# The first stage of a hybrid encoder layer in one written order, with 512 columns in a matmul of the dilated values

## The chip, the core and the metric

The kernel runs on one core of one Trainium2 chip. The metric is the device time of the program in microseconds; where several runs are compared, their median counts. Times inside the program come from one profiled execution.

## The reference

One layer of an encoder, for 1024 tokens of 1024 channels, all in float32. What matters here is that every branch starts from one normed input and one projection of it:

```python
h = rmsnorm(x, attn_norm_g)
proj = h @ w_in
(c_q, c_kv, k_rope, z_mla, q_dil, k_dil, v_dil, z_dil, g_mla, g_dil) = jnp.split(proj, split_points, axis=-1)
a_out = mla_attention(c_q, c_kv, k_rope, positions, ...)   # norms c_q and c_kv, then @ w_uq, @ w_ukv, rope, attention of 8 heads
d_out = dilated_mixture(q_dil, k_dil, v_dil, positions)    # 24 heads of 64 columns, three groups of 8
merged = sigmoid(g_mla + b) * ((a_out * silu(z_mla)) @ w_o_mla) + sigmoid(g_dil + b) * ((d_out * silu(z_dil)) @ w_o_dil)
out = rmsnorm(x + merged @ w_out, final_norm_g)
```

`c_q` has 256 columns, `c_kv` 128, `k_rope` 32, and `v_dil` 1536, which are three groups of 512.

## The kernel before, in words

**Precision.** Every float32 product is three matmuls (`mm3`, L144 to L146): high part by high part, high by low, low by high. An operand is cut in two by `split`: ScalarE (ACT in the profile) writes the rounded high part (L150), and VectorE (DVE) or GpSimd (POOL) subtracts it from the operand, which leaves the low part (L151). All DMAs leave through one queue, SyncE's (SP, L140), in program order.

**Stages.** The program has a first stage, then the block products (`blocks`, whose order is written out by hand: 16 items, each with 7 products of 12 matmuls by a Strassen-like scheme on halves of the tokens and of the contraction), then attention, gates and output. Only the first stage and the head of the block products are touched by the change.

**The first stage** consists of these pieces:

- `latent_proj`: `x` transposed comes in 16 loads, is scaled by the norm's gain and cut into high and low parts (`hTh`, `hTl`, which stay for the whole stage); 192 matmuls of 416 columns give `c_q`, `c_kv` and `k_rope` of 8 tiles of 128 tokens (`lat`). ACT sums the squares of the latent columns (L261, L262).
- `tables` computes sine and cosine tables and stores them to DRAM (`s_cs`); `table` loads them again, once for the latent heads (`cs_m`) and once for the dilated ones (`cs_d`).
- `token_factors`: ACT squares `x` in rows (L275), DVE works out the norm's factor of each token (`rcol`, L277), TensorE transposes it for a copy along the free axis (`R`).
- `up_weights` loads `w_uq` in two pieces and `w_ukv` in one through a staging tile `u_raw` that has one buffer, and splits each; the low parts (`uq_l`, `ukv_l`) are subtracted on POOL.
- `latents`, for each half of the tokens: DVE scales the `lat` tiles by the latent norm (L357), TensorE transposes them (L364), ACT and DVE write `lat_h` and `lat_l`, and 60 matmuls of 512 columns give the queries, keys and values of the latent heads. These leave by way of `mla_st` to DRAM.
- `dil_v`, six times (three groups, two quads of heads): one quad has 256 columns, so a token tile takes 8 steps of the contraction by 3 matmuls of 256 columns. The result is scaled by `rcol` on ACT (L445, L456) and DVE (L446) and stored.
- `block_sums`: sums and differences of the parts of `x` for the block products: 16 tiles `y` are loaded again, scaled by ACT (L473), combined on POOL (L475 to L478), and cut by ACT and DVE into `s_h` and `s_l`.

**What sets the order.** Inside the first stage a scheduler orders the instructions of each engine by their dependences and by the sequence in which the pieces are called. The pools have 6 PSUM buffers for `latent_proj` and `dil_v` (`NB_A`) and 2 for `latents`, so that matmuls of `dil_v` stand between those of `latents` on TensorE. At the end of the stage POOL combines the `y` tiles and splits the first operands (`w_l`) of the block products, again in an order that the scheduler chose. From `blocks` on, the order is the one in which the calls are written (`manual_schedule`): the operand of product j is split `LEAD` = 5 products ahead.

## Time and profile before

| | |
|---|---|
| median of three runs | 1254.29 us (1252.39 to 4276.14) |
| the profiled execution, its own time | 1254.46 us |
| its span in the trace | 1252.5 us, so about 2 us lie around it |
| PE busy in the span | 1212.4 us (97%) |
| first stage, until the first block product | 226.88 us |
| PE busy from 45 to 60 us, and from 60 to 80 us | 13.11 of 15 us, 12.50 of 20 us |
| PE busy from 80 to 220 us | all of 140 us |

A row of the timeline has the start and the duration of an instruction in us, its engine, its line in the kernel, the operation, the tiles it writes and reads, and in brackets how long its engine stood idle before it and what ended that. Matmuls overlap one another, so what one costs in a stream is the distance of the starts, not the duration in its row. A row of the groups has the count, the busy time, the mean of one in ns, and the idle time ahead. A row of the windows has, for each stretch, the time, then for each engine the busy time and the count, then TensorE's granted clock and the DMA share.

### The profile page before, as it was taken

To read this page: it belongs to the slowest core of one execution; us is meant where nothing else is said; L and a number is where in the kernel's file an instruction comes from. 1 tells how busy PE (TensorE), PEld (TensorE's weight loads), DVE (VectorE), ACT (ScalarE), POOL (GpSimd) and SP (SyncE) were. 2 spreads that over 40 slices of the span, in tenths; PEclk is the share of its full clock that TensorE was granted. 3 is DMA by queue.
4 is the path that set the end of the run, shared out by engine and by line. 5 is a ranking of instruction groups with operands and counts; after the bars stand their busy time and mean duration, and the time that the engine had idled before them with its cause. 6 is when DMAs were issued, how large, how long until landed. Compare 5 with 4: busy or idle time off the path is not lost.

```text
span 1252.5 us, 19486 instructions
## 1 busy us (share of the span) xinstructions
PE 1212.4 (97%) x6909; PEld 1064.5 (85%) x6909; DVE 730.8 (58%) x1304; ACT 622.0 (50%) x1300; POOL 570.2 (46%) x482
## 2 busy tenths in 40 slices
PE   8979999999999999999999999999999999999998
PEld 8979999888888888888888889878878888888886
DVE  7473534467657653345555575647766767759542
ACT  6534345444343344455554666545655656654232
POOL 2352218877777777543464442415521201168322
PEclk9989999999999999999999999899999999999999
DMA  9847589365445642496887898964634445225241
GB/s 333 225 157 283 196 302 317 103 180 156 135 132 165 174 127 100 122 268 197 233 257 200 207 294 212 266 175 116 178 128 119 110 118 135 85 96 182 84 151 51
DMA packets 126416, 221.37 MB, mean 177 GB/s; under 512 B 28072, under 2 KB 60400, under 8 KB 121392
## 3 DMA queue, kind: packets, MB, share of 16 engines
q1 hardware_dynamic: 126320, 220.14, 59.5%
q8 instruction: 54, 0.88, 0.3%
q14 instruction: 42, 0.34, 0.1%
HBM read 149.24 MB, written 70.85 MB: 176 GB/s over the span
## 4 chain that ended last, share of the span: by engine, by line
PE 75%; DMA 11%; DVE 4%; ACT 4%; issue 3%; POOL 1%; SPq 1%; ACTq 0%; POOLq 0%; DVEq 0%
PE bank L145 5%; PE bank L144 5%; PE bank L146 5%; PE pj L145 4%; PE bank L871 4%; PE pj L144 4%; PE pj L146 4%; DMA at_r<-s_dk 3%; PE st_a L144 2%; PE st_a L145 2%; PE st_d L145 2%; PE st_c L145 2%; PE st_d L146 2%; PE st_a L146 2%; PE st_c L146 2%
## 5 line engine op out<-in xcount | busy, mean ns | idle before, releaser
L151 POOL TENSOR_TENSOR w_l<-w_raw,w_h 128x512 fp32r<-128x512 f32 x188 | 247.5, 1330 | 276.7 <-ACT w_h L150 218.1
L150 ACT CAST w_h<-w_raw 128x512 fp32r<-128x512 f32 x188 | 112.6, 621 | 110.1 <-POOL w_raw L495 92.7
L144 PE MATMUL bank<-at_r,w_h 128*128 128x512 f32 x344 | 142.8, 415 | 0.0
L879 DVE TENSOR_TENSOR at_r<-bank,at_r 128x512 fp32r<-128x512 f32 x128 | 88.0, 688 | 84.5 <-ACT at_r L873 84.2
L145 PE MATMUL bank<-at_r,w_h 128*128 128x512 f32 x344 | 136.6, 397 | 0.6 <-POOL at_r L151 0.6
L146 PE MATMUL bank<-at_r,w_l 128*128 128x512 f32 x344 | 136.7, 397 | 0.0
L873 ACT CAST at_r<-bank 128x512 fp32r<-128x512 f32 x128 | 74.9, 586 | 72.5 <-PE bank L871 71.9
L145 PE MATMUL pj<-w_l,at_r 128*128 128x256 f32 x384 | 109.7, 286 | 0.0
L146 PE MATMUL pj<-w_h,at_r 128*128 128x256 f32 x384 | 109.6, 285 | 0.0
L144 PE MATMUL pj<-w_h,at_r 128*128 128x256 f32 x384 | 109.5, 285 | 0.0
L1137 ACT ACTIVATE at_f<-at_f,at_f 128x256 f32<-128x256 f32 x128 | 64.1, 502 | 52.1 <-DVE at_f L1130 51.8
L1156 DVE TENSOR_TENSOR at_r<-bank,at_r 128x512 fp32r<-128x512 f32 x64 | 43.9, 686 | 70.4 <-ACT at_r L1152 70.3
L495 POOL TENSOR_TENSOR w_raw<-w_raw 128x512 f32<-128x512 f32 x64 | 82.8, 1294 | 0.1
L871 PE MATMUL bank<-consts,at_f 128*128 128x128 f32 x512 | 77.2, 273 | 1.7 <-ACT at_f L863 1.1
L146 PEld LDWEIGHTS bank<-at_r,w_l 128*128 128x128 f32 x344 | 65.7, 191 | 14.9
L146 PEld LDWEIGHTS pj<-w_h,at_r 128*128 128x128 f32 x384 | 74.2, 193 | 1.0
L145 PEld LDWEIGHTS pj<-w_l,at_r 128*128 128x128 f32 x384 | 74.3, 193 | 0.7
L144 PEld LDWEIGHTS pj<-w_h,at_r 128*128 128x128 f32 x384 | 74.2, 193 | 0.7
L145 PEld LDWEIGHTS bank<-at_r,w_h 128*128 128x128 f32 x344 | 65.9, 192 | 9.9 <-POOL at_r L151 1.0
L144 PEld LDWEIGHTS bank<-at_r,w_h 128*128 128x128 f32 x344 | 65.8, 191 | 9.2
L895 PE MATMUL bank<-at_r,at_r 128*128 128x256 f32 x256 | 67.7, 285 | 1.3 <-ACT at_r L873 1.3
L896 PE MATMUL bank<-at_r,at_r 128*128 128x256 f32 x256 | 67.5, 285 | 0.9 <-DVE at_r L879 0.9
(321 smaller groups left out, 3325.3 us busy)
## 6 DMA issues: line engine op xcount, KB each, us to landing
w_raw<-wt SPq DMA_DIRECT2D x48, 512.0 KB, 3.7
at_r<-s_dq SPq DMA_DIRECT2D x32, 512.0 KB, 7.3
s_dk<-dq_st SPq DMA_DIRECT2D x80, 128.0 KB, 2.4
s_dv<-dv_st SPq DMA_DIRECT2D x32, 256.0 KB, 3.0
s_dq<-dq_st SPq DMA_DIRECT2D x64, 128.0 KB, 2.4
zt<-s_gt SPq DMA_DIRECT2D x32, 256.0 KB, 4.5
w_raw<-wv SPq DMA_DIRECT2D x12, 512.0 KB, 5.8
at_r<-s_dk SPq DMA_DIRECT2D x8, 576.0 KB, 11.3
```

Of the source, the lines that this page charges most:

```text
L144: mm(out, lh, rh, start=start, stop=False, skip_group_check=skip)
L145: mm(out, lh, rl, start=False, stop=False, skip_group_check=skip)
L146: return mm(out, ll, rh, start=False, stop=stop, skip_group_check=skip)
L150: self.nc.scalar.copy(out=h, in_=raw)
L151: sub.tensor_tensor(out=l, in0=raw, in1=h.bitcast(F32), op=ALU.subtract)
L495: self.nc.gpsimd.tensor_tensor(out=b[out], in0=b[x], in1=b[y], op=ALU.subtract)
L871: self.nc.tensor.transpose(pt[:, o:o + 128], self.P[k, b][:, 128 * kc:128 * kc + 128], self.ident)
L873: self.nc.scalar.copy(out=h, in_=pt)
L879: self.nc.vector.tensor_tensor(out=l, in0=pt, in1=h.bitcast(F32), op=ALU.subtract)
L895: mm(out, vv[:, kc], ph[:, x], start=kc == 0, stop=False)
L896: mm(out, vv[:, kc], pl[:, x], start=False, stop=kc == 7)
L1137: nc.scalar.activation(out=p, in_=p, func=AF.Exp, scale=-1.0, bias=nm, accum_out=den)
```

## The change

The whole first stage gets a written order as well (`first_stage`, under the same `manual_schedule` as `blocks`).

- **Dilated values.** A group's 512 columns are done at once. The work is 48 parts c = 0 to 47, 16 to a group; a part is 12 matmuls of 512 columns over half of the contraction for one token tile. Four tiles take their first half, then their second half, then the other four tiles; in group g the half whose operands are there comes first. 576 matmuls of 512 columns take the place of 1152 of 256. Each finished tile is taken by one ACT (L504) and one DVE (L505) instruction of 512 columns, and stored by one DMA.
- **Latent heads.** `latents` becomes a generator. From part 7 on, 1.5 of its 37 steps follow each part, and they are through after part 31. `latent_factors` does the norm's factors of all eight tiles at once, and the scalings of `lat` (`latent_scaled`, L387) stand behind parts 2 to 9. `up_weights` is called ahead of the parts, and its low parts are subtracted on DVE. `u_raw` keeps its one buffer. `mla_st` has 5 buffers in place of 2; PSUM is 4 and 4 buffers.
- **Sums behind.** `block_sums` is a generator that runs behind parts 32 to 42: two rounds of loads, then scaling, combining, and splitting of the round before. The `cs_d` tables are loaded at part 36, the first block weights at part 40, and their operands are split at parts 44 to 47.
- **Moved into the block products.** The four multiplications of `cs_d` by `R` on POOL, the four zero fills of `s_dq`, and the second block load. Operands of the block products change their pool every 4 products, not every one.

How this moves instructions is seen best at three places. The first is ACT just after the latent products, where the casts of the up weights stand. Names: `dv_st` is the staging tile of the dilated values, `lat_h` the transposed latents' high part. Before:

```order
L445 ACTIVATE dv_st<-pj,rcol 128x4x64 x5
L150 CAST uq_h<-u_raw 128x768
L445 ACTIVATE dv_st<-pj,rcol 128x4x64
L367 ACTIVATE lat_h<-pj,consts 128x512 x2
L445 ACTIVATE dv_st<-pj,rcol 128x4x64
L150 CAST w_h<-w_raw 128x512 x3
L150 CAST uq_h<-u_raw 128x768
L367 ACTIVATE lat_h<-pj,consts 128x512
```

And now:

```order
L279 ACTIVATE x_in,x_ss<-x_in 128x1024
L251 ACTIVATE x_junk,lat_ss<-pj 128x256
L251 ACTIVATE x_junk,lat_ss<-pj 128x128
L251 ACTIVATE x_junk,lat_ss<-pj 128x256
L251 ACTIVATE x_junk,lat_ss<-pj 128x128
L150 CAST uq_h<-u_raw 128x768 x2
L150 CAST ukv_h<-u_raw 128x1024
L504 ACTIVATE dv_st<-pj,rcol 128x8x64 x4
L406 ACTIVATE lat_h<-pj,consts 128x512 x3
```

The three casts, which stood apart between values that ACT was taking, now stand together, and the first four values (parts 4 to 7) are behind all three.

The second place is DVE at the same time. Before, the latent scalings follow the norm's factors, and the up weights are not on this engine:

```order
L208 SCALAR_TENSOR_TENSOR rs_u<-rs_u,lat_sc 128x8 x2
L209 SCALAR_TENSOR_TENSOR rs_y<-rs_u,rs_y 128x8 x2
L353 TENSOR_TENSOR rs_y<-rs_y,rcol 128x4 x4
L357 TENSOR_SCALAR lat<-lat,rs_y 128x256
L357 TENSOR_SCALAR lat<-lat,rs_y 128x128
```

Now the three subtractions of the up weights stand between them:

```order
L380 TENSOR_TENSOR rs_y<-rs_y,rcol 128x8 x2
L151 TENSOR_TENSOR uq_l<-u_raw,uq_h 128x768 x2
L151 TENSOR_TENSOR ukv_l<-u_raw,ukv_h 128x1024
L387 TENSOR_SCALAR lat<-lat,rs_y 128x256
L387 TENSOR_SCALAR lat<-lat,rs_y 128x128
L387 TENSOR_SCALAR lat<-lat,rcol 128x64
L387 TENSOR_SCALAR lat<-lat,rs_y 128x256
L387 TENSOR_SCALAR lat<-lat,rs_y 128x128
L387 TENSOR_SCALAR lat<-lat,rcol 128x64
L505 SCALAR_TENSOR_TENSOR dv_st<-pj,rcol,dv_st 128x8x64
```

So every scaling of `lat`, which the transposes on TensorE read, is behind the last of the up weights.

The third place is POOL at the end of the stage. Before, the combining of `y` (L475 to L478) and the splits of the first block operands alternate (L495 is a difference of block weights):

```order
L478 TENSOR_TENSOR y_1558<-y_1558,y_1555 128x512
L151 TENSOR_TENSOR w_l<-w_raw,w_h 128x512 x2
L495 TENSOR_TENSOR w_raw<-w_raw 128x512 x2
L151 TENSOR_TENSOR w_l<-w_raw,w_h 128x512 x2
L495 TENSOR_TENSOR w_raw<-w_raw 128x512
L475 TENSOR_TENSOR y_1588<-y_1585,y_1588 128x512
```

Now all 16 combinations come first. The last of them and what follows:

```order
L538 TENSOR_TENSOR y_1769<-y_1767,y_1769 128x512
L539 TENSOR_TENSOR y_1767<-y_1763,y_1767 128x512
L540 TENSOR_TENSOR y_1763<-y_1769,y_1763 128x512
L541 TENSOR_TENSOR y_1765<-y_1765,y_1763 128x512
L151 TENSOR_TENSOR w_l<-w_raw,w_h 128x512 x2
L648 TENSOR_TENSOR w_raw<-w_raw 128x512
L151 TENSOR_TENSOR w_l<-w_raw,w_h 128x512
L648 TENSOR_TENSOR w_raw<-w_raw 128x512
L151 TENSOR_TENSOR w_l<-w_raw,w_h 128x512
```

The operands of the first block products are therefore behind the last sum, where four of them were ahead of the last two rounds of sums.

The diff, cut to its core (added parts of `block_sums` that only repeat what was there are left out):

```diff
-NB_A = 6
+LATENTS_BEGIN, LATENTS_PACE = 7, 1.5
...
-    def latent_proj(self, lp, wl, xp, pj):
+    def first_products(self, lp, wl, xp, pools):
...
+                product(t, kc)
...
+        tables = self.tables(xp)
+        next(tables)
+        self.v_load(0, 0)
+        for i in range(4):
+            self.v_split(0, i)
+        for t in range(3):
+            squares(t)
+        taken(4)
+        next(tables)
+        self.v_load(0, 1)
+        for t in range(3, 5):
+            squares(t)
+        taken(5)
+        next(tables)
+        for t in range(5, 7):
+            squares(t)
+        for i in range(4):
+            self.v_split(1, i)
+        squares(7)
+        for t in range(6, 8):
+            taken(t)
+        run_all(tables)
...
+        v.tensor_copy(self.rcol, y)
...
+    def token_row(self, tp, pp):
...
-            self.split(raw[:, :n], uh[:, i] if i < 2 else kh, ul[:, i] if i < 2 else kl, nc.gpsimd)
+            self.split(raw[:, :n], uh[:, i] if i < 2 else kh, ul[:, i] if i < 2 else kl, nc.vector)
...
+    def latent_factors(self, tp):
...
+    def latent_scaled(self, t):
+        y, c = self.lat_f, self.lat[:, t]
+        for s, f in ((slice(0, 256), y[:, t:t + 1]), (slice(256, 384), y[:, 8 + t:9 + t]), (slice(384, 448), self.rcol[:, t:t + 1])):
+            self.nc.vector.tensor_scalar(out=c[:, s], in0=c[:, s], scalar1=f, scalar2=None, op0=ALU.mult)
...
-
+                    yield
...
+            yield
...
+            def stage():
+                return tp.tile([128, 2, 512], F32R, name="mla_st", bufs=5)
...
+            o = self.rope(pa, up_q(slice(640, 768)), cos, sin, tp)
+            yield
+                if j > 1:
+                    scaled(o[j - 2], self.qr[j - 2])
+                yield
...
-    def dil_v(self, g, quad, tp, pj):
...
+    def v_load(self, g, s):
+        if g == 3:
+            return
+        raws = self.v_raw[s] = [self.wp.tile([128, 2, 2, 256], F32, name="w_raw") for _ in range(2)]
+        for i in range(2):
+            for quad in range(2):
+                self.dma(raws[i][:, :, quad], self.a["wv"][2 * g + quad, s][:, 2 * i:2 * i + 2])
+    def v_split(self, s, i):
+        wp = (self.wp, self.wpx)[s]
+        h = wp.tile([128, 512], F32R, name="w_h", bufs=4)
+        l = wp.tile([128, 512], F32R, name="w_l", bufs=4)
+        self.split(self.v_raw[s][i // 2][:, i % 2].rearrange("p q c -> p (q c)"), h, l, self.nc.gpsimd)
+        self.v_w[s, i] = h, l
+    def v_part(self, c, pool, tp):
+        g, r = divmod(c, 16)
+        part, t = divmod(r, 4)
+        t += 4 * (part // 2)
+        s = (0, 1, 1, 0)[part] ^ (g & 1)
+        begin = part % 2 == 0
+        if begin:
+            self.v_ps[t] = pool.tile([128, 512], F32, name="pj")
+        ps = self.v_ps[t]
+        sl = slice(128 * t, 128 * t + 128)
+        for i in range(4):
+            kc = 4 * s + i
+            self.mm3(ps, self.hTh[:, kc, sl], self.hTl[:, kc, sl], *self.v_w[s, i], begin and i == 0, not begin and i == 3)
+        if begin:
+            return
+        nc = self.nc
+        pv = ps.rearrange("p (h d) -> p h d", d=64)
+        f = self.rcol[:, t:t + 1]
+        if g < 2:
+            st = tp.tile([128, 8, 2, 64], F32R, name="dv_st")
+            nc.scalar.mul(st[:, :, 0], pv, f)
+            nc.vector.scalar_tensor_tensor(out=st[:, :, 1], in0=pv, scalar=f, in1=st[:, :, 0].bitcast(F32), op0=ALU.mult, op1=ALU.subtract)
+            if g == 0:
+                dst = self.dv[0][128 * t + 64:128 * t + 192]
+                dst = self.dv[1].rearrange("(r m) x -> m r x", r=4)[32 * t:32 * t + 32]
+            self.dma(dst, st.rearrange("p h a d -> p (h a d)"))
+        else:
+            st = tp.tile([128, 8, 64], F32, name="dv_st")
+            nc.scalar.mul(st, pv, f)
+            self.dma(self.dv[2][:, 128 * t:128 * t + 128].rearrange("a t x -> t a x"), st.rearrange("p (a h) d -> p a (h d)", h=2))
...
+        loads(0)
+        loads(1)
+        yield
+        scaled(0)
+        yield
+        for kc in range(4):
+            added(kc)
+            if kc:
+                parts(kc - 1)
+                if kc < 3:
+                    loads(kc + 1)
+            yield
+            if kc < 3:
+                scaled(kc + 1)
+            yield
+        parts(3)
+    def first_stage(self, cp, dpool, sums):
+        tc, nc = self.tc, self.nc
+        self.v_raw, self.v_w, self.v_ps, self.blk, self.opd = {}, {}, {}, {}, {}
+        with ExitStack() as ctx, ExitStack() as left, ExitStack() as inner:
+            pool = lambda stack, name, bufs=1, **k: stack.enter_context(tc.tile_pool(name=name, reuse_waits="tile", bufs=bufs, **k))
+            pl = pool(ctx, "pj_l", 4, space=PSUM)
+            pj = pool(ctx, "pj_a", 4, space=PSUM)
+            vp = pool(ctx, "dvp", 3, side="right")
+            lp = pool(left, "lp")
+            with ExitStack() as stack:
+                wl, xp = pool(stack, "wl"), pool(stack, "xp", 3)
+                self.first_products(lp, wl, xp, (pj, pl))
+            mpool, up, tp = pool(left, "cosm"), pool(left, "up"), pool(left, "lt", 2)
+            self.cos_m, self.sin_m = self.table(mpool, "cs_m", 32)
+            self.latent_factors(tp)
+            weights = self.up_weights(up)
+            latents = self.latents(weights, up, tp, pl)
+            steps, later = 0.0, None
+            for c in range(48):
+                self.v_part(c, pj, vp)
+                g, r = divmod(c, 16)
+                if 2 <= c < 10:
+                    self.latent_scaled(c - 2)
+                if c == 20:
+                    self.token_row(vp, pl)
+                first, second = (0, 1) if g & 1 else (1, 0)
+                if r == 6:
+                    self.v_load(g + 1, first)
+                if r == 14:
+                    self.v_load(g + 1, second)
+                if g < 2 and 12 <= r < 15:
+                    for i in ((0, 1), (2,), (3,))[r - 12]:
+                        self.v_split(first, i)
+                if g and r < 3:
+                    for i in ((0, 1), (2,), (3,))[r]:
+                        self.v_split(1 - (g & 1), i)
+                if c >= LATENTS_BEGIN and latents:
+                    steps += LATENTS_PACE
+                    while steps >= 1 and latents:
+                        steps -= 1
+                        try:
+                            next(latents)
+                        except StopIteration:
+                            latents = None
+                            left.close()
+                            sp = pool(sums, "sums")
+                            z = self.zero = sp.tile([128, 512], F32, name="zero")
+                            nc.gpsimd.memset(z, 0.0)
+                            later = self.block_sums(sp, pool(inner, "bs"))
+                elif later:
+                    next(later, None)
+                if c == 36:
+                    self.cos_d, self.sin_d = self.table(dpool, "cs_d", 0)
+                if c == 40:
+                    self.block_loads(0, self.block_items[0], (self.wp, None))
+                if c >= 44:
+                    for j in ((0, 1), (2,), (3,), (4,))[c - 44]:
+                        self.block_minus(j, self.block_items)
+                        self.block_operand(j, self.block_items)
+            run_all(later)
+            self.block_minus(LEAD, self.block_items)
+            for r in (0, S + 64):
+                for p in range(2):
+                    self.dma(self.dk[0][:, p, :, :, r:r + 64].rearrange("h c x t -> (c x) h t"), z[:64].rearrange("p (h t) -> p h t", t=64))
+                self.dma(self.dv[0][r:r + 64].rearrange("r (a b) -> (r a) b", b=512), z)
...
-            wp = (self.wp, self.wpx)[j % 2]
+            wp = (self.wpx, self.wp)[j // 4 % 2]
...
-        for n in range(2):
-            self.block_loads(n, items[n])
-        for i in range(4):
-            self.dma(self.dq[2][i].rearrange("e c r h (a b) f m -> (e c r) (h a) (b f m)", a=2), self.zero.unsqueeze(1).to_broadcast([128, 4, 512]))
-        for j in range(LEAD):
-            self.block_minus(j, items)
-            self.block_operand(j, items)
-        self.block_minus(LEAD, items)
-        with self.tc.manual_schedule():
...
+        self.block_loads(1, items[1], pools)
+        for x in range(1, places + 14):
...
+            if x in (2, 3, 4, 5):
+                y, c = (self.cos_d, self.sin_d)[x // 2 - 1], slice(512 * (x % 2), 512 * (x % 2) + 512)
+                self.nc.gpsimd.tensor_tensor(out=y[:, c], in0=y[:, c], in1=self.R[:, c], op=ALU.mult)
...
+            if x in (4, 8, 12, 16):
+                i = x // 4 - 1
+                self.dma(self.dq[2][i].rearrange("e c r h (a b) f m -> (e c r) (h a) (b f m)", a=2), self.zero.unsqueeze(1).to_broadcast([128, 4, 512]))
...
+                self.first_stage(cp, dpool, sums)
```

288 lines of the change are left out of this document (114 added, 174 removed).

## The prediction

> **What bounds the kernel now.** The page comes first: TensorE is busy almost throughout, and only the first three slices of 40 (31.3 us each) are below 9 for its own reasons.
>
> ```profile
> PE 1212.4 (97%) x6909; PEld 1064.5 (85%) x6909; DVE 730.8 (58%) x1304; ACT 622.0 (50%) x1300; POOL 570.2 (46%) x482
> PE   8979999999999999999999999999999999999998
> ```
>
> So time is won on TensorE alone: fewer or cheaper matmuls, or less standing idle in the first stage. The windows say where it stands (time, then busy time and count of PE, PEld, DVE, ACT, POOL, granted clock, DMA share, GB/s).
>
> ```profile
> 45.00:60.00 15.00, 13.11 (x111) 12.91 (x110) 7.88 (x45) 4.81 (x15) 1.70 (x2) 1.00 1.01 248
> 60.00:80.00 20.00, 12.50 (x85) 12.00 (x84) 14.56 (x44) 5.18 (x10) 7.57 (x6) 0.74 0.36 119
> 80.00:200.00 120.00, 120.00 (x895) 114.83 (x895) 53.97 (x82) 51.64 (x95) 39.61 (x30) 1.00 0.72 257
> 200.00:220.00 20.00, 20.00 (x170) 20.00 (x168) 7.56 (x7) 10.00 (x19) 16.93 (x13) 1.00 0.88 326
> 220.00:240.00 20.00, 19.04 (x108) 16.58 (x107) 8.03 (x7) 10.85 (x23) 15.95 (x11) 1.00 0.47 155
> ```
>
> Between 80 and 220 us nothing is left to fill. The one large hole is at 60 to 80 us. The timeline of PE names the five stops (the last column says how long PE stood and for what) and gives the starts of matmuls from which I take what one costs.
>
> ```profile
> 5.77 0.71 PE L144 MATMUL pj<-wl_h,at_r 128*128 128x416 f32 x1 [5.77 <-ACT wl_h L150]
> 44.15 0.28 PE L144 MATMUL pj<-w_h,at_r 128*128 128x256 f32 x1
> 53.86 0.27 PE L279 MATMUL pj<-consts,rs_y 128*8 128x128 f32 x1 [1.89 <-DVE rs_y L209]
> 71.38 0.69 PE L364 MATMUL pj<-consts,lat 128*128 128x128 f32 x2 [6.81 <-DVE lat L357]
> 73.39 0.47 PE L364 MATMUL pj<-consts,lat 128*128 128x128 f32 x1 [0.69 <-DVE lat L357]
> 80.31 0.60 PE L364 MATMUL pj<-consts,lat 128*128 128x128 f32 x4
> 80.66 0.36 PE L146 MATMUL pj<-w_h,at_r 128*128 128x256 f32 x1
> 213.76 0.28 PE L146 MATMUL pj<-w_h,at_r 128*128 128x256 f32 x1
> 225.64 0.28 PE L146 MATMUL pj<-w_h,at_r 128*128 128x256 f32 x1
> 226.88 0.50 PE L144 MATMUL st_a<-at_r,w_h 128*128 128x512 f32 x1 [0.96 <-ACT dv_s L456]
> 229.74 0.39 PE L144 MATMUL st_b<-at_r,w_h 128*128 128x512 f32 x1
> 232.46 0.39 PE L144 MATMUL st_c<-s_h,w_h 128*128 128x512 f32 x1
> ```
>
> From 213.76 to 225.64 there are 99 matmuls of 256 columns: 0.120 us each. From 229.74 to 232.46 there are 12 of 512: 0.227 each, 2.72 for the twelve. Four transposes take 0.35.
>
> **The budget of the stage before**, from the first value matmul (44.15) to the first block product (226.88), is 182.7 us: 1152 x 0.120 = 138.2 for the values; 120 x 0.227 = 27.2 for the latent heads; 32 transposes 2.8; stops of 1.89 + 6.81 + 0.69 + 0.96 = 10.4; and 4.1 that remain. Of these some 2.5 are a half clock:
>
> ```profile
> 68.00:71.40 3.40, 0.02 (x1) 0.03 (x1) 3.40 (x5) 0.35 (x1) 3.40 (x4) 0.50 0.00 0
> 74.00:76.00 2.00, 2.00 (x11) 2.00 (x10) 2.00 (x9) 0.39 (x1) 0.00 (x0) 0.50 0.00 0
> 77.40:80.00 2.60, 2.60 (x24) 2.60 (x24) 1.38 (x3) 1.77 (x4) 0.80 (x1) 1.00 0.89 282
> ```
>
> After the long stop the granted clock stays at 0.50 for about 5 us of work. By the Trainium skill (TensorE: Matmul & The Clock Gate, on the clock gate) an idle window of some microseconds halves the clock until the array has been busy about as long; these rows agree, with one stop of 6.81 us. A longer stop costs no second such toll.
>
> **The wider matmuls.** 1152 x 0.120 = 138.2 become 576 x 0.227 = 130.6, which is 7.6 us less, all of it on TensorE. Bounds: nothing, if a 512 costs two 256s, and 576 x (0.240 - 0.227) = 7.6 by these rows. I take the rows: the stationary side is a 128 x 128 tile of `at_r` in the values as in the block products. The Trainium skill (same page, Back-to-back issue gap) gives an isolated warm matmul as columns / 2.4 + 2.5 ns; by that a pair of 256 and one 512 differ by 2.5 ns, an estimate of 1.5 us for the whole edit. The measured 0.120 is well over what the formula has for 256, so I follow the row.
>
> **The latent heads' start.** Here the order bites. The latent products end near 44.2 as before. Parts 0 to 7 run to 44.2 + 8 x 2.72 = 65.9. Behind part 7 come the first transposes, and they read `lat` tiles that DVE scales only after all three subtractions of the up weights. `u_raw` has one buffer, so the loads form a ladder: a load, ACT's cast, DVE's subtraction, and only then the next load. Its rungs by the rows of before:
>
> ```profile
> L140 SPq DMA_DIRECT2D u_raw<-wuq x2: 398/412/426, 62.3 to 77.6; - x2
> L150 ACT CAST uq_h<-u_raw x2: 832/836/839, 67.1 to 81.3; 128x768 fp32r<-128x768 f32 x2
> L150 ACT CAST ukv_h<-u_raw x1: 1052/1052/1052, 89.7 to 89.7; 128x1024 fp32r<-128x1024 f32 x1
> DMA to landing us min/median/max: 4.3/4.6/4.8
> L151 DVE TENSOR_TENSOR wl_l<-wl_raw,wl_h 128x416 fp32r<-128x416 f32 x4 | 2.3, 580 | 0.0
> s_qn<-mla_st SPq DMA_DIRECT2D x8, 512.0 KB, 3.0
> 53.84 0.17 DVE L277 COPY rcol<-rs_y 128x8 f32<-128x8 f32 x1
> 56.73 0.36 DVE L349 SCALAR_TENSOR_TENSOR lat_sc<-lat_ss,rcol 128x4 f32<-128x4 f32 x4
> ```
>
> - A DVE subtraction of 768 columns, from the 416-column row by width: 0.58 x 768 / 416 = 1.07; of 1024: 1.43.
> - The first one. `rcol` was there at 54.0 before. In the new order ACT has all squares, four value casts and the sines of the tables ahead of `taken(7)`, and the cosines' store and four loads of `cs_m` are ahead of `u_raw` on SP: I put `rcol` at 57 and the factors at 60.5 (17 small operations of about 0.2). The first load is there by then, and its subtraction ends at 61.5.
> - Two more rungs. Landing between 3.0 (the 512 KB store) and 4.8 (this load before); with little else on the queue I take 3.9. So 3.9 + 0.84 + 1.07 = 5.8, and 3.9 + 1.05 + 1.43 = 6.4: the last subtraction ends at 73.7 (72 to 75.5).
> - Then four scalings of about 1.0 each (16 long and 8 short ones, whose row follows) and two takings of values of 0.7:
>
> ```profile
> 69.89 6.39 DVE L357 TENSOR_SCALAR lat<-lat,rs_y 128x256 f32<-128x256 f32 x16
> L151 DVE TENSOR_TENSOR mla_st<-pj,mla_st 128x512 fp32r<-128x512 f32 x16 | 11.1, 692 | 23.2 <-ACT mla_st L150 23.2
> ```
>
> The transposes can start at S = 73.7 + 4.0 + 1.4 = 79.1. PE is at 65.9, so it **stands 13.2 us** where before it stood 6.81 + 0.69. It cannot go round this: the values of parts 4 to 7 wait on ACT behind the same three casts, and their PSUM buffers are the ones that part 8 needs.
>
> **The rest of the stage.** From S: 40 parts x 2.72 = 108.8; latents 27.2; transposes 2.8; the 4.1 that remained before, half clock included. S + 142.9 = 222.0. The stop for the tokens' transpose (1.89) is gone, since part 20 is long after `rcol`.
>
> **The tail.** The first sums can be loaded when the latents have left their pool, behind part 31, near 179. The rows of before for this chain:
>
> ```profile
> DMA to landing us min/median/max: 3.5/5.8/8.5
> L473 ACT ACTIVATE y<-y,consts x16: 708/720/725, 186.0 to 221.1; 128x512 f32<-128x512 f32 x16
> L477 POOL TENSOR_TENSOR y<-y,y x4: 1301/1624/1694, 192.2 to 223.2; 128x512 f32<-128x512 f32 x4
> L151 DVE TENSOR_TENSOR s_l<-y,s_h 128x512 fp32r<-128x512 f32 x16 | 20.3, 1298 | 27.7 <-ACT s_h L150 27.3
> 182.17 4.32 SPq L140 DMA_DIRECT2D y<-xt  x8
> 189.44 1.30 POOL L475 TENSOR_TENSOR y<-y,y 128x512 f32<-128x512 f32 x1 [5.19 <-ACT y L473]
> ```
>
> From load to first combination 7.3 us: 187. A round on POOL is four operations of 1.30 to 1.62, 6.0; rounds 0 and 1 end at 193 and 199. Rounds 2 and 3 need buffers that DVE's splits free at 194.5 and 200.5, then 5.8 of landing and 2.9 of scaling: combined by 210 and 217. The first block operand then is split by 218.5 and the second by 220, against a TensorE that arrives at 222. That cover is 3.5 us for the first operand and 4.7 for the second (needed 2.72 later); without it each us late is a us lost. With the wait of 0.96 for the last value, which stays, I put 1.5. The first block product then starts at 223.5, against 226.88.
>
> Moved at no cost: POOL's four multiplications of `cs_d` (some 5 us) and the zero fills go into a stretch where POOL is busy 15.95 of 20 us and five operands ahead; uncovered they would cost up to 5 us. Values' splits have 16 us of parts behind which their 5.3 us of POOL fit.
>
> **Sum.** 226.88 - 223.5 = 3.4 us less in the profiled execution: 1254.46 - 3.4 = 1251.1; the median of before lies 0.2 lower, so **1250.9 us**. In parts: 7.6 from the wider matmuls and 1.9 from the tokens' transpose, less 5.7 more idle at the latents and 0.5 at the tail.
>
> **The rivals.**
> - Quick loads. If `u_raw` lands in 3.0 and `rcol` comes at 54 as before, S is 79.1 - 1.8 - 3.0 = 74.3: 1246.1. For it, DMA share falls to 0.36 in that window; against it, no `u_raw` landed under 4.3. By the Trainium skill (DMA: Bandwidth & Descriptors, Anatomy of one DMA) 384 KB would take 2.0 us plus bytes over 436 GB/s, an estimate of 2.9; the trace shows 4.3 to 4.8.
> - Fully hidden. If the latents never stop TensorE: 13.2 and some 2.5 of half clock less, 1235. The ladder speaks against it: even with landings of 3.0 it ends after 65.9.
> - Slower: the sums come late. The second and third rounds land at 8.5 (the slowest `y` of before), twice 2.7, and splits and combinations slow each other as in the row of 1.62 (once more 3): the first operand is split at 227 and 5 operands then come at POOL's pace of 2.6 each. TensorE waits 5 at once and 2 to 3 more: 1259. It decides once POOL's last combination ends after 220.5. For it: the operands are behind all sums; against it: the rows' medians end 3.5 us earlier.
> - The change does not do what it says: a 512 costs two 256s. Then 7.6 are missing, 1258.5.
>
> **How the numbers follow.** Forecast 0.60, with a range of its own from 1247 to 1255; quick loads 0.13; hidden 0.04; late sums 0.19; no gain by width 0.04. The range of 8 in 10 takes in the quick loads and most of the late sums: 1242 to 1259. A measurement of this kernel tells 2%, 25 us, from no change: below 1229.2 only if the latents are hidden and more goes well (0.03), above 1279.4 only if the moved work starves the block products (0.03); within, 0.94.
>
> **What would show it.** Right: value matmuls 0.227 apart; one PE stop of 11 to 15 us between 64 and 81, ended by DVE's scaling of `lat`; in it three `u_raw` loads, each issued behind a DVE subtraction; no stop at the tokens' transpose; the first block product at 221 to 226. Wrong: that stop under 7 us, or a stop of over 4 us at the head of the block products ended by `w_l` on POOL, or PE stops inside the 40 parts that I have at none.

## The result and the profile after

The changed kernel took 1273.63 us (median of 4 runs, 1271.86 to 1274.65) against 1253.93 us of the kernel before in the same measurement: a ratio of 1.0162, 95% interval 1.0141 to 1.0183. One of the four runs of the kernel before took 4276.14 us, for a reason that no trace shows; the others lie between 1252.4 and 1254.3, and the ratio leaves it out. The change is slower by 1.6%; the forecast was 1250.9 us and a range up to 1259. The span of the profiled execution is 1272.1 us against 1252.5.

TensorE's starts, laid side by side from the two traces, say where the 19.3 us lie. The table splits the program at four places that both kernels have: the first block product, the second of the 16 items of block products, the last block product, and the first wait of the attention for its keys.

| us | before | after | difference |
|---|---|---|---|
| until the first block product | 226.88 | 231.18 | +4.3 |
| first item of the block products | 19.18 | 26.93 | +7.7 |
| 15 further items | 285.4 | 285.4 | 0 |
| last block product until the attention's first wait for keys | 67.7 | 72.4 | +4.7 |
| from there to the last matmul | 646.9 | 649.5 | +2.6 |

The windows after, in the same columns as before:

```profile
45.00:60.00 15.00, 15.00 (x68) 12.42 (x67) 5.83 (x19) 11.23 (x28) 5.06 (x4) 1.00 0.72 203
60.00:80.00 20.00, 9.43 (x38) 6.93 (x37) 10.78 (x40) 4.45 (x6) 0.00 (x0) 0.74 0.33 104
160.00:200.00 40.00, 37.11 (x151) 29.78 (x150) 11.06 (x15) 18.42 (x32) 16.59 (x14) 0.91 0.71 251
220.00:240.00 20.00, 15.89 (x59) 12.13 (x58) 9.93 (x8) 10.85 (x19) 13.47 (x10) 0.83 0.37 122
240.00:260.00 20.00, 17.05 (x70) 13.66 (x69) 4.38 (x7) 5.75 (x11) 17.87 (x15) 0.91 0.80 276
```

The hole at 45 to 60 is closed, the one at 60 to 80 is still there, and three new ones have come, each with a granted clock below 1. The timeline of PE names them:

```profile
75.96 1.05 PE L403 MATMUL pj<-consts,lat 128*128 128x128 f32 x2 [8.84 <-issue]
77.82 0.48 PE L403 MATMUL pj<-consts,lat 128*128 128x128 f32 x1 [0.81 <-DVE lat L387]
79.10 0.48 PE L403 MATMUL pj<-consts,lat 128*128 128x128 f32 x1 [0.80 <-DVE lat L387]
192.55 0.79 PE L144 MATMUL pj<-w_h,at_r 128*128 128x512 f32 x1 [2.34 <-ACT w_h L150]
226.97 0.39 PE L145 MATMUL pj<-w_l,at_r 128*128 128x512 f32 x1
227.20 0.39 PE L146 MATMUL pj<-w_h,at_r 128*128 128x512 f32 x1
231.18 0.79 PE L144 MATMUL st_a<-at_r,w_h 128*128 128x512 f32 x1 [3.59 <-ACT w_h L150]
251.21 0.80 PE L144 MATMUL st_c<-s_h,w_h 128*128 128x512 f32 x1 [2.95 <-ACT st_c L679]
560.54 0.50 PE L146 MATMUL bank<-at_r,w_l 128*128 128x512 f32 x1 [2.46 <-POOL w_l L151]
```

Values at 512 columns are 0.227 apart, as priced. The stop at the latents is there too. What was not in the sum are the stops at 192, 251 and 560, and most of the one at 231. Each of the first three in time drags a second loss behind it: the first start behind the stop comes 0.59 later and 5 to 11 after it 0.43 apart instead of 0.227, 1.4 to 2.7 us more.

**The head** has the forecast's mechanism. The tile view of the staging buffer, and then DVE's first scalings of `lat`:

```profile
L140 SPq DMA_DIRECT2D u_raw<-wuq x2: 351/359/367, 56.9 to 64.8; - x2
...
L151 DVE TENSOR_TENSOR uq_l<-u_raw,uq_h x2: 949/954/960, 63.9 to 68.9; 128x768 fp32r<-128x768 f32 x2
L151 DVE TENSOR_TENSOR ukv_l<-u_raw,ukv_h x1: 1226/1226/1226, 74.4 to 74.4; 128x1024 fp32r<-128x1024 f32 x1
DMA to landing us min/median/max: 3.2/3.2/3.2
```

```profile
75.52 0.54 DVE L387 TENSOR_SCALAR lat<-lat,rs_y 128x256 f32<-128x256 f32 x2
```

Three rungs, each load behind a subtraction. The first subtraction ends at 64.8 instead of my 61.5 and the last at 75.6 instead of 73.7; landings of 3.2 instead of 3.9 make up part of the delay. But TensorE does not wait for the four scalings and two takings that I put behind the ladder at 5.4 us. Its first transposes start at 75.96, behind the scaling of one tile (the profile names no releaser for that wait; the scaling at 75.52 is the work that ends just before), and two later ones wait 0.8 each for theirs. So TensorE's idle is 10.45 us in three pieces against my 13.2. The formula that the prediction takes from the Trainium skill (DMA: Bandwidth & Descriptors, Anatomy of one DMA) for its 2.9 us is given there for transfers that GpSimd issues. These loads leave through SyncE's queue, and the 3.2 here is what they took.

**The stop at 192** comes from ACT's order. The cast of the last operand that the values need stands behind a scaling of `y` that waits for its load:

```profile
191.27 0.72 ACT L534 ACTIVATE y<-y,consts 128x512 f32<-128x512 f32 x1 [1.70 <-DMA y<-xt]
191.90 0.60 ACT L150 CAST w_h<-w_raw 128x512 fp32r<-128x512 f32 x1
```

**The tail** did not go as forecast. The sums come in four rounds, each of four loads, four scalings, four combinations and four splits. Who waits for whom, from ACT's timeline and then POOL's (the scaling of `y` at 209.61 is the last of the third round):

```profile
209.61 0.72 ACT L534 ACTIVATE y<-y,consts 128x512 f32<-128x512 f32 x1 [1.68 <-DMA y<-xt]
210.81 2.17 ACT L150 CAST s_h<-y 128x512 fp32r<-128x512 f32 x4
230.52 1.12 ACT L150 CAST w_h<-w_raw 128x512 fp32r<-128x512 f32 x2
```

```profile
193.80 1.28 POOL L538 TENSOR_TENSOR y<-y,y 128x512 f32<-128x512 f32 x1
204.66 1.28 POOL L541 TENSOR_TENSOR y<-y,y 128x512 f32<-128x512 f32 x1
210.41 1.29 POOL L538 TENSOR_TENSOR y<-y,y 128x512 f32<-128x512 f32 x1 [4.47 <-ACT y L534]
223.01 1.30 POOL L538 TENSOR_TENSOR y<-y,y 128x512 f32<-128x512 f32 x1 [6.21 <-ACT y L534]
227.78 1.59 POOL L541 TENSOR_TENSOR y<-y,y 128x512 f32<-128x512 f32 x1
231.20 3.35 POOL L151 TENSOR_TENSOR w_l<-w_raw,w_h 128x512 fp32r<-128x512 f32 x2 [1.82 <-ACT w_h L150]
```

POOL has combined the second round at 205.9, but ACT casts its parts (which frees the buffers of the fourth round) only from 210.81, since these casts stand behind the scaling of the third round, which waits for its loads until 209.6. So the fourth round's loads leave at 214, and the last combination ends at 229.4 where I had 217. Behind it comes the first block operand. The first round was late too: its first combination starts at 193.8, where I had 187. Its first load left at 180.0, but the second only at 185.2, since SP waited 3.6 us for the landing of the latents' last store (`s_mv` in the waits below), and the last scaling of that round waited for its load until 191.3.

The stop at 251 has its cause on SP. From its waits between 178 and 245 us (in total, times, longest), then its timeline, then ACT's:

```profile
SPq L140 <- ACT dv_st L514: 26.6, 6, 10.3
SPq L140 <- DMA s_mv<-mla_st: 3.6, 1, 3.6
```

```profile
230.64 10.03 SPq L140 DMA_DIRECT2D s_dv<-dv_st  x4
244.89 4.32 SPq L140 DMA_DIRECT2D w_raw<-wt  x4
```

```profile
250.05 0.62 ACT L150 CAST w_h<-w_raw 128x512 fp32r<-128x512 f32 x1 [2.55 <-DMA w_raw<-wt]
```

The stores of the last values wait 10 us for ACT (L514), whose last takings stand between the casts of the block operands, which wait for POOL. The second block's weights, which the change moved behind these stores, leave at 244.9; ACT waits for them in its order until 250, and the copy that TensorE needs (L679) is behind that wait.

### The profile page after: what moved, and what is told of

Same layout as the page of the kernel before. It is cut to its first block, busy times and chain, and to the rows that moved or that the text cites. A ratio compares the mean times of both kernels' runs of the same rounds, so it can differ in the third digit from the quotient of the medians.

```text
span 1272.1 us, 18198 instructions
## 1 busy us (share of the span) xinstructions
PE 1218.1 (96%) x6333; PEld 1041.6 (82%) x6333; DVE 726.5 (57%) x1273; ACT 616.6 (48%) x1276; POOL 561.6 (44%) x479
## 4 chain that ended last, share of the span: by engine, by line
PE 70%; DMA 15%; POOL 6%; issue 4%; DVE 2%; ACT 2%; SPq 2%; POOLq 0%; ACTq 0%; DVEq 0%
PE bank L146 5%; PE bank L145 5%; PE bank L144 5%; PE bank L1020 3%; PE pj L145 3%; PE pj L146 3%; PE pj L144 3%; DMA at_r<-s_dk 3%; PE st_c L144 2%; PE st_c L146 2%; PE st_c L145 2%; PE st_d L146 2%; PE st_d L144 2%; PE st_a L144 2%; PE st_a L145 2%
## 5 line engine op out<-in xcount | busy, mean ns | idle before, releaser
L144 PE MATMUL pj<-w_h,at_r 128*128 128x512 f32 x192 | 77.6, 404 | 2.5 <-ACT w_h L150 2.3
L145 PE MATMUL pj<-w_l,at_r 128*128 128x512 f32 x192 | 76.7, 400 | 0.6 <-POOL w_l L151 0.6
L146 PE MATMUL pj<-w_h,at_r 128*128 128x512 f32 x192 | 76.5, 398 | 0.0
L1020 PEld LDWEIGHTS bank<-consts,at_f 128*128 128x128 f32 x512 | 59.7, 141 | 3.1 <-ACT at_f L1012 1.5
L151 POOL TENSOR_TENSOR at_r<-at_f,at_r 128x512 fp32r<-128x512 f32 x25 | 36.1, 1452 | 49.5 <-ACT at_r L150 49.5
L1044 PEld LDWEIGHTS bank<-at_r,at_r 128*128 128x128 f32 x256 | 48.7, 190 | 9.2 <-ACT at_r L1022 3.0
```

The source lines that it names most:

```text
L144: mm(out, lh, rh, start=start, stop=False, skip_group_check=skip)
L145: mm(out, lh, rl, start=False, stop=False, skip_group_check=skip)
L146: return mm(out, ll, rh, start=False, stop=stop, skip_group_check=skip)
L151: sub.tensor_tensor(out=l, in0=raw, in1=h.bitcast(F32), op=ALU.subtract)
L1020: self.nc.tensor.transpose(pt[:, o:o + 128], self.P[k, b][:, 128 * kc:128 * kc + 128], self.ident)
L1044: mm(out, vv[:, kc], ph[:, x], start=kc == 0, stop=False)
```

## The experiments

Twelve kernels ran, on four chips. The totals come from one execution each, but for c_best (median of ten) and c_final (median of six). On the same chip the kernel before took 1251.8 beside e_ladder, e_parts, e_oper and e_alt, 1261.1 beside e_ladder2, e_pace, c_pas and c_all, 1254.1 beside c_nopace, c_best and c_w256, and 1253.5 beside c_final. So the stage times decide, each from one profiled execution. They differ little from chip to chip: the 15 further items take 285.4 to 285.7 in every kernel but e_oper (289.3). The last value matmul starts at 226.3 to 227.7 in the changed kernel and the three whose edits lie behind most of the values (e_parts, e_oper, e_alt), so differences of about 1 us are not read.

| us | first block product | first item | to the attention's wait | rest | total |
|---|---|---|---|---|---|
| after | 231.2 | 26.9 | 72.4 | 649.5 | 1273.6 |
| e_ladder | 230.8 | 28.0 | 71.5 | 644.4 | 1268.6 |
| e_ladder2 | 218.1 | 27.5 | 72.0 | 651.2 | 1262.7 |
| e_parts | 226.6 | 23.7 | 71.4 | 645.2 | 1260.7 |
| e_oper | 234.4 | 22.1 | 72.2 | 646.7 | 1273.3 |
| e_alt | 230.6 | 27.5 | 68.5 | 647.8 | 1268.3 |
| e_pace | 246.5 | 19.0 | 72.3 | 649.8 | 1281.6 |
| c_pas | 228.0 | 19.1 | 68.3 | 652.7 | 1262.2 |
| c_all | 226.8 | 19.0 | 69.3 | 644.3 | 1253.4 |
| c_nopace | 214.7 | 19.6 | 68.2 | 648.7 | 1245.5 |
| c_best | 210.8 | 27.5 | 68.4 | 645.1 | 1247.7 |
| c_w256 | 214.3 | 26.3 | 67.3 | 647.8 | 1249.6 |
| c_final | 210.3 | 21.8 | 68.2 | 645.0 | 1240.9 |

The column "rest" holds the attention and the output, which no edit touches. It runs from 644.3 to 652.7, so the 2.6 us that the changed kernel loses there are within what it varies by among these executions.

### The ladder of the up weights

e_ladder spreads the three pieces, each with its load:

```diff
-        for i in range(3):
+        def piece(i):
...
+                if c in (5, 8):
+                    piece(c // 4)
```

> The changed kernel with one edit: the second and third load-and-split of the up weights stand behind parts 5 and 8 instead of ahead of part 0, so that the scalings of lat and the first takings of values are no longer behind the whole u_raw ladder. Theory A (the ladder makes the 9.2 us gap of TensorE starts at 66.7 to 76.0, and the sums at the end start when the latents end, so that the whole rest of the stage moves with it): gap of 3 us or less, no half clock behind it, first block product 9 to 13 us earlier than 231.2, total 1260 to 1264 us. Rival B (the end of the stage is set by something that does not follow from the head, such as the loads): the gap goes, but the first block product stays at 229 or later and the total at 1270 or more.

The gap went from 76 and came back at 87.5. From ACT's timeline in e_ladder:

```profile
85.83 1.04 ACT L150 CAST ukv_h<-u_raw 128x1024 fp32r<-128x1024 f32 x1 [10.78 <-DMA u_raw<-wukv]
86.78 1.26 ACT L408 ACTIVATE lat_h<-pj,consts 128x512 fp32r<-128x512 f32 x2
```

A cast that waits is a wait for everything written behind it on its engine: here the latents' high parts stand behind a load that left at 78.4, because on SP it was behind value stores and other loads. The kernel does not decide between the theories; it moved the stop. So a second form sends each load at once and moves only the split:

```diff
+        def cut(i):
+            self.split(raws[i], uh[:, i] if i < 2 else kh, ul[:, i] if i < 2 else kl, nc.vector)
+            if i < 2:
+                load(i + 1)
...
+                if c in (6, 10):
+                    cut(c // 4)
```

> The changed kernel with the up weights spread once more, with the load of each piece sent right behind the split of the one before it, and only the splits moved: the second behind part 6, the third behind part 10. In the first try ScalarE stood 8.7 and 10.8 us in its casts for loads that had been sent too late, and TensorE's gap came back at 87.5. Theory A (the gap is ScalarE and VectorE standing in order behind the ladder, and goes when the loads are sent early and the splits late): no stop over 2 us between 60 and 100, last value matmul 9 to 13 us earlier than 227.2, total 1260 to 1265. Rival B (the one buffer makes a chain that only moves): a stop of 5 us or more between 65 and 100, total 1268 or more.

Theory A holds. The only stop left there, and the next that TensorE meets, in e_ladder2:

```profile
67.77 0.33 PE L411 MATMUL pj<-consts,lat 128*128 128x128 f32 x1 [0.85 <-DVE lat L395]
179.98 0.49 PE L144 MATMUL pj<-w_h,at_r 128*128 128x512 f32 x1 [3.05 <-ACT w_h L150]
```

The last value matmul is at 213.65 instead of 227.20, the first block product 13.1 us earlier. The losses at the tail stay as they were (a stop of 4.1 ahead of the first block product, and 27.5 for the first item), so the tail follows the latents and is a loss of its own.

### The sums

```diff
-            if kc:
-                parts(kc - 1)
-                if kc < 3:
-                    loads(kc + 1)
+            if kc == 1:
+                for i in range(2):
+                    parts(i)
+                    loads(i + 2)
+            if kc == 3:
+                parts(2)
```

> The changed kernel with one edit in the sums: the splits of round 1 and the loads of round 3 stand ahead of the scaling of round 2, not behind the combination of round 2. Theory A (ScalarE's order makes a ladder of the rounds: the splits that free the y buffers of round 3 stand behind a scaling that waits for the y of round 2): the loads of round 3 leave near 207 to 211 instead of 214 to 219, POOL's last combination ends at 222 to 225 instead of 229.4, the first block product starts at 226 to 229 instead of 231.2, total 1265 to 1270. Rival B (the landing of y or POOL's own pace sets the end): last combination at 228 or later, total within 1.5 us of 1272.

Theory A: the last combination ends at 221.1, a little earlier than expected. POOL in e_parts combines the fourth round right behind the third, and ACT casts the first block operands 7.5 us earlier than after the change:

```profile
213.48 1.29 POOL L541 TENSOR_TENSOR y<-y,y 128x512 f32<-128x512 f32 x1
214.74 1.29 POOL L538 TENSOR_TENSOR y<-y,y 128x512 f32<-128x512 f32 x1
```

```profile
223.01 1.14 ACT L150 CAST w_h<-w_raw 128x512 fp32r<-128x512 f32 x2 [0.63 <-DMA w_raw<-wt]
```

The first block product follows the last value matmul by 0.23, and the first item loses 3.3 us less. The stop at 251 is now at 243, 2.73 long. The total is 12.9 us less, of which 4.3 lie in the part that no edit touches. Of the 12.4 us by which POOL was later than forecast, the edit takes away 8.2; the 4.1 that stay are the first round's lateness.

The other way to get the sums out of the tail is to start them sooner:

```diff
-LATENTS_BEGIN, LATENTS_PACE = 7, 1.5
+LATENTS_BEGIN, LATENTS_PACE = 7, 2.0
```

> The changed kernel with one number changed: two steps of the latent heads behind each part instead of 1.5, so that they are through after part 25 and the sums can start six parts (some 16 us) earlier. Theory A (the end of the stage is set by when the sums start, since their loads need the latents' memory): POOL's last combination at 213 to 219 instead of 229.4, first block product within 1 us of the last value matmul, no stop at 251, total 1256 to 1263. Rival B (the latent heads themselves are too slow for that pace, and TensorE stops between parts 8 and 25 for what it gains later): new stops of 4 us or more between 80 and 160, total 1267 or more.

Neither: the total is in rival B's range, but the stops of 4 us or more stand behind 180 us and not between 80 and 160. The latents bore the pace, and the block products started without a stop behind the last value and ran their first item in 19.0; but TensorE lost 20 us more than in the changed kernel before that. From its timeline in e_pace, and POOL's:

```profile
188.09 0.79 PE L145 MATMUL pj<-w_l,at_r 128*128 128x512 f32 x1 [5.61 <-POOL w_l L151]
210.60 0.80 PE L145 MATMUL pj<-w_l,at_r 128*128 128x512 f32 x1 [6.61 <-POOL w_l L151]
```

```profile
184.78 1.59 POOL L541 TENSOR_TENSOR y<-y,y 128x512 f32<-128x512 f32 x1
186.33 3.39 POOL L151 TENSOR_TENSOR w_l<-w_raw,w_h 128x512 fp32r<-128x512 f32 x2
```

Sums that start at part 26 stand on POOL between the splits of the values' operands (parts 28 to 34), and each split then waits for a round of combinations. The tail's loss has only changed its place.

### The block operands and the second block's weights

```diff
-                if c >= 44:
-                    for j in ((0, 1), (2,), (3,), (4,))[c - 44]:
-                        self.block_minus(j, self.block_items)
-                        self.block_operand(j, self.block_items)
+            for j in range(LEAD):
+                self.block_minus(j, self.block_items)
+                self.block_operand(j, self.block_items)
             run_all(later)
```

> The changed kernel with one edit: the casts and splits of the first five block operands stand behind part 47, not between parts 44 to 47. Theory A (the last takings of values on ScalarE wait behind the casts of the block operands, which wait for POOL; SP waits for them 10 us, and the second block weights leave only at 244.9, which makes TensorE's stop at 251.2): the last taking at 228 to 231 instead of 239.6, the second block weights leave at 232 to 238, the stop at 251 (3.3 us and some 1.5 of half clock) goes, the first item takes 21 to 23 us instead of 26.9, total 1266 to 1269. Rival B (the stop at 251 is POOL's pace of the operands): the stop stays at 2 us or more, total within 1.5 us of 1272.

SP in e_oper:

```profile
230.88 3.36 SPq L140 DMA_DIRECT2D s_dv<-dv_st  x4
238.46 13.17 SPq L140 DMA_DIRECT2D w_raw<-wt  x4
```

The mechanism is theory A's: the last taking is at 233.2 instead of 239.6, the weights leave 6.4 us earlier, the stop at 251 is gone and the first item takes 22.1. The total is rival B's, because the price was left out of the expectation: the operands themselves are now behind four takings of values, the first block product starts 3.2 us later, and the second item has a stop of 1.95 and takes 22.9 instead of 19.0. The 14 us in which POOL makes the first five operands and their differences have to lie somewhere.

### The pools of the operands

```diff
-            wp = (self.wpx, self.wp)[j // 4 % 2]
+            wp = (self.wpx, self.wp)[(j // 4 if j < 8 else j) % 2]
```

> The changed kernel with one edit: from the ninth product on, the block operands change their pool at every product, as in the kernel before, not at every fourth. Theory A (the last operands of the block stage wait for buffers, POOL's markers that release memory to the attention stand behind them, loads leave late and TensorE stops at 560.5): no stop over 1 us there, the attention starts about 4 us earlier against the end of the block products, total 1267 to 1269.5. Rival B (that stop is a matter of when transfers happen to land): still a stop of 2 us or more near there, or one further on in its place, total within 1.5 us of 1272.

Theory A: no stop of PE near 560, the way to the attention 68.5 instead of 72.4. POOL at the end of the block products, in the changed kernel and then in e_alt:

```profile
536.26 1.29 POOL L151 TENSOR_TENSOR w_l<-w_raw,w_h 128x512 fp32r<-128x512 f32 x1 [5.11 <-ACT w_h L150]
540.22 0.26 POOL L1431 MEMSET area<- 1x1 f32 x6
558.33 0.09 POOL L1431 MEMSET area<- 1x1 f32 x1 [13.52 <-DMA s_gt<-dq_st]
```

```profile
534.26 2.54 POOL L151 TENSOR_TENSOR w_l<-w_raw,w_h 128x512 fp32r<-128x512 f32 x2 [3.10 <-ACT w_h L150]
536.74 0.09 POOL L1431 MEMSET area<- 1x1 f32 x1
554.98 0.09 POOL L1431 MEMSET area<- 1x1 f32 x1 [10.17 <-DMA s_gt<-dq_st]
```

With four operands in a row from one pool, the casts of the next stage's first weights wait for TensorE's last products. POOL's markers (L1431), with which memory passes to the attention, stand behind them; the attention's loads leave 3.5 us later and meet the gates' stores, whose landing POOL awaits before it splits what TensorE needs.

### Together

c_pas puts e_parts, e_alt and one more edit together; this one takes the casts of the last group's operands out from behind the scaling of `y`, which made the stop at 192.6:

```diff
-                if g and r < 3:
-                    for i in ((0, 1), (2,), (3,))[r]:
+                if g and r == 0:
+                    for i in range(4):
                         self.v_split(1 - (g & 1), i)
```

> Three edits together on the changed kernel: the sums' order of e_parts (1260.7 alone), the pools of e_alt (1268.3 alone), and all four splits of the last group's second half of operands behind part 32, so that no cast of them stands behind the scaling of y. Theory A (the three losses are separate: tail, end of the block products, and the stop at 192.6): the stop at 192 and its half clock go, last value matmul at 219 to 222, first block product at 223 to 226 (the sums now set it, since their last combination is at 221), total 1252 to 1257. Rival B (they are one loss that is counted three times): total 1259 or more.

The stops at 192, 251 and 560 are gone, but another came in PE's timeline of c_pas, and the first block product stands at 228.0, not 223 to 226:

```profile
205.98 0.80 PE L144 MATMUL pj<-w_h,at_r 128*128 128x512 f32 x1 [4.46 <-ACT dv_st L514]
```

Part 40 needs a PSUM buffer that ACT frees by taking a value, and that taking stands behind the casts of the sums' parts. So the total of 1262.2 is in rival B's range, by a new loss and not because the three were one: each of the three stops is gone. An engine that no longer waits at one place waits at the next.

> All edits that take a wait away: c_pas, e_ladder2 and two latent steps a part. Theory A: 44.2 + 48 x 2.72 + 27.2 + 2.8 = 204.7 for TensorE's own work, with no stop over 2 us until the block products; first block product at 206 to 213, no stop at 251, total 1234 to 1243, faster than the kernel before by 1 to 1.5%. Rival B (TensorE that runs ahead makes the sums, POOL or the loads of the stage the bound): first block product at 216 or later, total 1246 or more.

Rival B, by the stops of e_pace (5.62 at 176.9): first block product at 226.8, total 1253.4. Without the faster pace:

> c_pas and the spread up weights of e_ladder2 together, the latent heads at their old pace of 1.5 steps. Theory A (the losses at the head and at the tail are separate, and the pace alone made the stops of 5.6 us and less that c_all and e_pace show at the value operands): no stop at the latents, first block product 12 to 14 us earlier than the 228.0 of c_pas, so 214 to 216; the stop for the takings of values (4.5 us in c_pas) stays; total 1244 to 1250. Rival B: first block product at 220 or later, total 1253 or more.

As expected: first block product at 214.7, no stop over 0.95 at the latents, total 1245.5, and the stop for the takings (3.19) is there. The next edit aims at it:

```diff
-                self.v_part(c, pj, vp)
+                self.v_part(c, pl if c >= 40 else pj, vp)
```

> c_nopace, and parts 40 to 47 write the four PSUM buffers that the latent heads have left, so that they need not wait for ScalarE's takings of parts 36 to 39, which stand behind the splits of the sums. Theory A (the stop of 4.5 us in c_pas is that PSUM wait): no stop over 1 us from 70 us to the block products, last value matmul at 205 to 210, first block product at 209 to 213 (the sums set it), total 1236 to 1246 and 0.5 to 1.3% faster than before on the same chip. Rival B (ScalarE's lateness only moves to the first block product): first block product at 214 or later, no gain over c_nopace.

Between the two. The PSUM wait goes (last value matmul 207.1, first block product 210.8), yet the first item takes 27.5 again: rival B's lateness, inside the first item. The median of ten runs, 1247.7, misses theory A's 1236 to 1246 and is no gain over c_nopace. It is 0.9957 of the kernel before (0.9936 to 0.9978). The last edit follows from it:

```diff
-            self.split(..., self.nc.gpsimd)
+            self.split(..., self.nc.vector if j < LEAD else self.nc.gpsimd)
...
-                if c >= 44:
-                    for j in ((0, 1), (2,), (3,), (4,))[c - 44]:
-                        self.block_minus(j, self.block_items)
+                if c == 44:
+                    for j in range(2):
                         self.block_operand(j, self.block_items)
+            for j in range(2, LEAD):
+                self.block_minus(j, self.block_items)
+                self.block_operand(j, self.block_items)
```

> c_best with two more edits at its last loss, the 8.5 us that its first item of block products takes too long (27.5 instead of 19.0): the low parts of the first five operands are subtracted on VectorE, which is idle there from 211 to 225, instead of POOL, and the third to fifth operand stand behind the takings of the last values. Theory A (POOL's pace and ScalarE's takings behind it make the stops of 3.3, 0.6 and 2.3 us and the half clock behind them): first block product at 209 to 212, first item 19 to 22 us, total 4 to 9 us less than c_best, 1237 to 1243 on a chip where the kernel before takes 1254. Rival B (the second block weights, whose load left at 223.8, set the first item): first item at 24 us or more, total within 2 us of c_best.

Theory A: 1240.94 us (median of six, 1239.08 to 1242.12), 0.989 of the kernel before (1253.49), interval 0.9855 to 0.9925. What each of the two edits is worth was not separated. They also let the second block weights leave earlier, at 217.2 instead of 223.8; but the three stops of c_best had ended by 219.3, before that load left, so rival B does not account for them. DVE's row for the third to fifth operand and PE's stop in c_final:

```profile
214.20 3.98 DVE L151 TENSOR_TENSOR w_l<-w_raw,w_h 128x512 fp32r<-128x512 f32 x3 [1.82 <-ACT w_h L150]
```

```profile
210.34 0.50 PE L144 MATMUL st_a<-at_r,w_h 128*128 128x512 f32 x1 [2.61 <-ACT w_h L150]
```

### The width alone

c_w256 is c_best with two matmuls of 256 columns in place of one of 512. Its values are not the reference's, and only its time is read.

```diff
-            self.mm3(ps, ...)
+            for x in (slice(0, 256), slice(256, 512)):
+                self.mm3(ps[:, x], ...)
```

> c_best with the values' matmuls at 256 columns again (1152 of them in the same order): the width alone. Theory A (0.120 us for 256 and 0.227 for 512, and TensorE sets the stage): last value matmul 6 to 8 us later than in c_best, total 4 to 8 us more. Rival B (a 512 costs two 256s, or TensorE does not set the stage): less than 2 us between them in either.

The last value matmul in c_best, then in c_w256:

```profile
207.10 0.39 PE L146 MATMUL pj<-w_h,at_r 128*128 128x512 f32 x1
```

```profile
213.85 0.28 PE L146 MATMUL pj<-w_h,at_r 128*128 128x256 f32 x1
```

It is 6.75 us later, theory A's 6 to 8. The first block product is 3.5 us later, the attention's first wait 1.2. The span is 1247.9 against 1243.9, but 2.8 of these 4.0 lie in the part that no edit touches. So the width is worth on TensorE what its rows say, and most of it is lost again while the sums stand at the end; theory A's 4 to 8 us of total are not shown.

## Why the prediction was wrong

The mechanism at the head was right and its size too high. Two steps of the sum failed: that TensorE has no stop within the 40 parts, and that the sums of the tail follow their dependences alone. Two costs were not in the sum at all: the place of the second block's weights, and the operands' change of pool.

Against the forecast, in the profiled executions: the head took 3.1 us less, the rest of the stage 8.6 more, the wait ahead of the first block product 2.3 more and the first operands behind it 3.3, the stop at 251 another 4.5, the way to the attention 4.7, and the part behind it 2.6. That makes the 22.7 us by which the forecast was short.

- **The wider matmuls** (7.6 us): right. 0.227 apart in the trace after; 6.75 us by c_w256, where the 40 of 48 parts behind the first transposes differ by 40 x 24 x (0.120 - 0.1133) = 6.4.
- **The latent heads' start** (TensorE stands 13.2): the mechanism is right, the ladder and its rungs as told; the size was 10.45, since the transposes start behind one tile's scaling and not behind four. That the ladder makes the stop is shown by e_ladder2, where it goes.
- **The tokens' transpose** (1.89): right, no stop there.
- **The rest of the stage** (S + 142.9, no stop within): wrong by 8.6 us: the last value matmul ended at 227.4, 151.5 after the first transposes at 76.0. By the starts 6.3 of it lie between 188 and 200, the stop at 192 with its half clock: a scaling of `y` that waits for its load is written ahead of the cast of the values' last operand. c_pas shows it, since the stop goes with the cast's place, while it stays in e_parts and e_alt, the other two edits of c_pas. Right behind the first transposes the waits of 0.8 and the half clock cost 5.2, where the sum had 4.1 for the whole rest; the remainder is in short waits.
- **The tail** (1.5): the mechanism failed. "Rounds 2 and 3 need buffers that DVE's splits free at 194.5 and 200.5" (rounds counted from 0) read the dependence and not the order: the second of these splits stands on ACT behind the scaling of round 2. POOL ended at 229.4 instead of 217, later than the 220.5 from which the rival of the late sums decides. That rival had the place and nearly the price there (5 at once and 2 to 3 more; it was 3.6 and 3.3), but not the cause: it has the second and third rounds land at 8.5, and of rounds 2 and 3 no landing that the trace has took over 5.3. e_parts shows the order to be the cause of 8.2 of the 12.4 us; the other 4.1 come from the first round, which the sum had at 187 and which waited on SP for a store to land.
- **"Moved at no cost"**: wrong for the second block's weights. I named the multiplications and the zero fills and left out that load, which is moved past the last value stores and the zero fills on SP. It cost the stop at 251, some 4.5 us with its half clock (e_oper takes it away).
- **Not priced at all**: the operands' change of pool every four products, 3.9 us by e_alt at the end of the block products, 300 us behind the change's place.
- Of the difference, 2.6 us lie in the attention, within what that part varies by; no cause is claimed for them.

So 7.6 and 1.9 us were won, about 26 lost in five places and 2.6 behind them; of the five the sum had only the latents and a small part of the tail. Four of the five have a common cause, shown by e_ladder2, c_pas, e_parts and e_oper: with a written order, an instruction that waits on ACT, POOL or SP holds everything written behind it, of whatever stage. The fifth, at 560, is one of buffers and what stands behind their release. The Trainium skill (TensorE: Matmul & The Clock Gate, in its table of properties) calls the queues of ScalarE and VectorE strict FIFO; the traces agree, and in e_ladder ScalarE's wait of 10.78 is the plainest case.

## What to carry to other kernels

Where an order is written out, list for each engine and each DMA queue the instructions that wait for a transfer or for another engine, and look at what stands behind each of them, whatever it belongs to: a load is sent early, and its consumer is written where the traces show it landed. Dependences give the earliest time only; walk the tail of a stage row by row in the order of each engine before giving a price. After taking one wait away expect the next in the same chain, and judge an edit by stage times rather than by the total, which one unrelated part can move by several us.

## What was not expected of the hardware

In all kernels together TensorE made 29 stops of 1.9 to 4.5 us between 60 us and the attention's first wait for its keys. After 25 of them starts of matmuls of 512 columns lay 0.43 apart, instead of 0.227, mostly for 4 to 13 matmuls, which is 0.8 to 2.6 us on top; after four they did not (2.60 us at 548 in e_ladder2 is the longest). So the length of a short stop does not tell whether a half clock follows, and one that follows can cost as much as the stop itself. The half clock comes in pieces of about 3.4 us: in the changed kernel the granted clock is 0.50 from 192.6 to 199.4 and from 250.6 to 254.0, and 1.00 in the 3.4 us behind each. The forecast's "a longer stop costs no second such toll" missed that several short ones each may.

While VectorE subtracted the low parts of the sums and POOL combined, both slowed: VectorE's took 0.68 us alone and up to 1.78 beside POOL, and POOL's combinations 1.28 alone and up to 1.74, as the rows of before already had it.
